# A hybrid encoder layer: which ring of buffers a pair's expert choices use, where the expert activations are loaded, integer positions, and late gate steps with priority

## The chip, the cores and the metric

The kernel runs on one core of one Trainium2 chip. The metric is the device time of one execution in microseconds (us), the median of several runs. The profile is a trace of one execution. Its engines are PE (TensorE's matmuls; PEld its weight loads), DVE (VectorE), ACT (ScalarE), POOL (GpSimd) and SP (SyncE, which here only issues transfers). Each runs its instructions in program order.

## The reference

One layer: a token-mixing part (convolution and RWKV-7 heads), then a retrieval of single-neuron experts. The cut below is the second part, in which the change lies; S = D = 1024, 8 heads, 128 keys per half, 16 choices per head, 16384 experts.

```python
h2 = adaln(x, shift2, scale2)
q = (h2 @ peer_wq).reshape(bsz, seq, PEER_HEADS, PEER_QDIM)
s1 = jnp.einsum('bshd,hnd->bshn', q[..., :half], peer_k1)
s2 = jnp.einsum('bshd,hnd->bshn', q[..., half:], peer_k2)
v1, i1 = lax.top_k(s1, PEER_TOPK)
v2, i2 = lax.top_k(s2, PEER_TOPK)
cand = (v1[..., :, None] + v2[..., None, :]).reshape(bsz, seq, PEER_HEADS, PEER_TOPK * PEER_TOPK)
sc, ci = lax.top_k(cand, PEER_TOPK)
experts = (jnp.take_along_axis(i1, ci // PEER_TOPK, axis=-1) * PEER_NKEYS
           + jnp.take_along_axis(i2, ci % PEER_TOPK, axis=-1))
gates = jax.nn.softmax(sc, axis=-1)
u_sel = jnp.take(peer_u, experts, axis=0)
act = jax.nn.gelu(jnp.einsum('td,tkd->tk', h2, u_sel), approximate=False) * gates
y2 = jnp.einsum('tk,tkd->td', act, jnp.take(peer_v, experts, axis=0))
x = layer_norm(ALPHA * x + gate2[:, None, :] * y2, ln2_g, ln2_b)
```

## The kernel before

Tokens go in eight tiles of 128, and through the middle of the kernel in four pairs of tiles (256 tokens). Up to about 530 us the modulation and the input projection run, then the RWKV recurrence over 16 chunks, into which work of the pairs that are done is filled. For a pair, `front` is the output projection (L186, evicted by ACT at L796) and the layer norms, and `query` computes the queries: `to_channels` turns the normed tokens into `h2hi` and `h2lo` (PE L220, ACT L222), then come 16 query tiles in four groups of four. A query tile is 24 matmuls (L186) with a 1 MB block of split weights, `wsplit`, which `load_split` loads at L170 into one of three buffers; ACT evicts it as `qt` (L858). After each group PE forms the key scores (L863) from the group's four evictions, and ACT evicts them (L866).

For tiles 0 to 5, `choose` then finds the 16 experts of each head from the scores. DVE forms the candidates (L904) and searches them (L767 to L771); ACT copies the positions from integers to floats (L912); DVE turns positions into two indices (L913 to L930, L955, L958 to L960); ACT casts indices (L935) and takes the exp (L956); DVE compares (L940) and POOL multiplies and sums (L943, L949, L951) to pick the chosen keys, and `put` sends them to `sel_d` (L932). Choices take their tiles of 2 KB ("pages") from a ring: up to here the ring `pg`, of 31 pages, which the query's `qt`, `s12`, keys and `hf` use as well.

Tiles 0 to 4 are handled densely: `gate_matrix` reads `sel_d` back (L973), transposes it (L979), and in 32 steps of four tokens builds a matrix of gates over all experts (DVE L991 and L995, POOL L997, ACT L1000 and L1001, PE L1003, eviction L1004), written to `G_d` by DMA (L1011). Tiles 5 to 7 gather their experts' rows by DMA. The expert loop (32 groups of experts) multiplies the 640 dense tokens' activations `h2h` and `h2l` with the expert weights (L1227), applies gelu and gates (L1229 to L1233), multiplies back (L1261) and adds up (L1266), beside which POOL and DVE work through the gathers (L1145, L1153, L1160). The choices of tiles 6 and 7 run there too (`choose_late`).

Between recurrence and expert loop lies a loop (L1067 on) that steps the last pair's `front`, the third pair's `query` and the last pair's `query`, with a step of the choices every second pass and a step of the gates every twelfth (`TSLOW`, `TGATE`). The last pair's `front` takes its pages from a second ring, `pg2`, of 20 pages (`NP2`). Behind the loop that ring is closed, and its memory goes to the pool `dp` with `h2h` and `h2l`, which 16 transfers (L1080) load from `h2t_d`.

The order of each engine's instructions is not written out: a scheduler with a time model lists them as their inputs come ready in the model, in order of priority, and this order is then fixed.

Of the kernel before, what the change touches and what calls it, by code (L numbers as in the profile page):

```python
# [10 lines left out]
F32 = mybir.dt.float32  # L11
F32R = mybir.dt.float32r
BF = mybir.dt.bfloat16
I32 = mybir.dt.int32
U32 = mybir.dt.uint32
AF = mybir.ActivationFunctionType
OP = mybir.AluOpType
# [4 lines left out]
S = 1024  # L22
D = 1024
KD = 8
CW = 512
KS = 31
NH = 8
# [13 lines left out]
PB = 256  # L41
# [13 lines left out]
WRAW = 2  # L55
WSPLIT = 3
RUN = 4
NP2 = 20
PIN = 3
STEPS = 4, 3  # L60
# [20 lines left out]
def layer_kernel(ctx, tc, x, cols, c_row, cond_w, w_in, w2a2, g2, w_out, ln_rows, wq, keys, peer_u, peer_ut, peer_v, peer_vt, out):  # L81
    nc = tc.nc
    V, A, G, T = nc.vector, nc.scalar, nc.gpsimd, nc.tensor
    ld = nc.sync.dma_start
# [26 lines left out]
    dt = lambda shape, name, n: [dram.tile(shape, F32, name=f"{name}{i}") for i in range(n)]  # L111
# [9 lines left out]
    h2t_d = dram.tile([2, KD, 128, ND], F32, name="h2t_d")  # L121
    sel_d = dt([3, 128, 128], "sel_d", 8)
    score_d = {t: [dram.tile([128, 512], F32, name=f"score_d{t}_{g}") for g in range(4)] for t in range(6, 8)}
    split_d = {}

    GPART = [(0, ND // TB - 4), (ND // TB - 4, ND // TB - 1), (ND // TB - 1, ND // TB)]
    G_d = [dram.tile([32, 128, b - a, 4 * TB], F32, name=f"G_d{a}") for a, b in GPART]
# [28 lines left out]
    def page(name, dt=F32, w=512):  # L156
        return pgp.tile([128, max(w, 512)], dt, tag="pg", name=name)[:, :w]
# [6 lines left out]
    def load_split(src, j):  # L164

        both = ws.tile([128, 2, KD, 128], F32R, name="wsplit", bufs=WSPLIT)
        hi, lo = both[:, 0], both[:, 1]
        key = src.tensor.name, j
        if key in split_d:
            ld(both.bitcast(F32), split_d[key])  # L170
        else:
            raw = load_raw(src[j])
            A.activation(hi, raw, AF.Copy)  # L173
            G.tensor_sub(lo, raw, hi.bitcast(F32))  # L174
            split_d[key] = dram.tile([128, 2, KD, 128], F32, name=f"split_{key[0]}{j}")
            ld(split_d[key], both.bitcast(F32))
        return hi, lo
# [50 lines left out]
    def step(jobs):  # L228
        while jobs:
            try:  # L230
                next(jobs[0])
                return
            except StopIteration:
                jobs.pop(0)
# [212 lines left out]
    slow, gates, gb, conv_left, psg, selbank = [], [], [], [], [], [None]  # L447
# [108 lines left out]
    for l in range(6):  # L556
# [6 lines left out]
        nm = rc.tile([128, 64], F32, name=f"offm{l}", bufs=1)  # L563
# [9 lines left out]
    side, rate, credit, fills = [], [0.0], [0.0], [0]  # L573

    def fill():

        credit[0] += rate[0]
        fills[0] += 1
        if credit[0] >= RUN:
            credit[0] -= RUN  # L580
            for _ in range(RUN):
                step(side)
# [9 lines left out]
            fn(hi_, q)  # L592
            fill()

    kept, ys, late, normed = {}, {}, [], {}

    def quad(name, bufs=3):
        return rw.tile([128, 4, 64], F32, name=name, bufs=bufs)
# [229 lines left out]
    def query(t0):  # L828

        n, nt, tile0 = PB, PB // 128, t0 // 128  # L830
        fetch = [tile0 + t in GT for t in range(nt)]
        xn = normed.pop(t0)
        hi, lo = duo("h2hi", F32R)[1], duo("h2lo", F32R)[1]

        def keep(k, h, l):
            for w, f in enumerate((h, l)):
                for t in range(nt):
                    if not fetch[t]:
                        d = 128 * DT.index(tile0 + t)
                        ld(h2t_d[w, k, :, d:d + 128], f[:, 128 * t:128 * t + 128].bitcast(F32))  # L840

        to_channels(xn, lambda k: mod[:, 24 + k:25 + k], lambda k: modp[:, k, 1:2], hi, lo, keep)
        yield
        vi = [page("vi").rearrange("p (q h a r) -> p q h a r", q=2, h=NH, a=2) for t in range(nt)
              if tile0 + t not in score_d]
        val = [t[:, 0] for t in vi]
        idx = [t[:, 1].bitcast(U32) for t in vi]
        for g in range(4):
            kt = pgp.tile([128, 4, 128], F32, tag="pg", name="keys")
            ld(kt, keys[:, 4 * g:4 * g + 4, :])  # L850
            qt = []
            for m in range(4):
                w = load_split(wq, 4 * g + m)
                pt = mm(n)
                yield from proj(w, (hi, lo), pt)
                if m % 2 == 0:
                    qp = page("qt").rearrange("p (a t) -> p a t", a=2)
                A.activation(qp[:, m % 2, :], pt, AF.Copy)  # L858
                qt.append(qp[:, m % 2, :])
            for t in range(nt):  # L860
                ps = mm()
                for m in range(4):
                    T.matmul(ps[:, 128 * m:128 * m + 128], qt[m][:, 128 * t:128 * t + 128], kt[:, m, :],  # L863
                             start=True, stop=True)
                s = page("s12")
                A.activation(s, ps, AF.Copy)  # L866
                if tile0 + t in score_d:
                    ld(score_d[tile0 + t][g], s)
                    yield
                    continue  # L870
                for m in range(4):
                    best16(val[t][:, 2 * g + m // 2, m % 2], idx[t][:, 2 * g + m // 2, m % 2], s[:, 128 * m:128 * m + 128])
                    yield
        for t in range(len(vi)):
            slow.append(choose(tile0 + t, val[t], idx[t], 0, NH, 4, lambda nm, d, w: page(nm, d, w), G))

    def choose_late(tt, lt):

# [10 lines left out]
    def choose(tt, val, idx, h0, nh, nb, new, E):  # L889
# [2 lines left out]
        sh3 = [128, nh, TOPK]  # L892
        quad = lambda nm, dt=F32: new(nm, dt, 4 * n).rearrange("p (q h r) -> p q h r", q=4, h=nh)
        qf, qg, qu = quad("tkf"), quad("tkg"), quad("tku", U32)
        fp, m1, m2, m3 = (qf[:, i] for i in range(4))
        top, shf, fo = qg[:, 0], qg[:, 1], (qg[:, 2], qg[:, 3])
        pos = qu[:, 0]
        shi, qi_, ri_ = (qu[:, i].bitcast(I32) for i in (1, 2, 3))
# [10 lines left out]
                best16(top[:, h], pos[:, h], cand[:, h - hh, :])  # L909
                yield  # L910

        A.activation(fp, pos, AF.Copy)  # L912
        V.tensor_scalar(m1, fp, 32.0, None, op0=OP.is_ge)  # L913
        V.tensor_scalar(m2, fp, 48.0, None, op0=OP.is_ge)
        V.tensor_scalar(m3, fp, 64.0, None, op0=OP.is_ge)
        yield
        V.tensor_add(shf, m1, m2)
        V.scalar_tensor_tensor(shf, m3, 2.0, shf, op0=OP.mult, op1=OP.add)
# [8 lines left out]
        qb = new("tkb", BF, 8 * n).rearrange("p (q h r) -> p q h r", q=8, h=nh)  # L927
        isel, jsel = qb[:, 0], qb[:, 1]
        V.scalar_tensor_tensor(isel, m1, -2.0, qi_, op0=OP.mult, op1=OP.add)
        V.tensor_sub(jsel, fp, ri_)  # L930
        yield
        put = lambda w, t: ld(sel_d[tt][w][:, h0 * TOPK:h0 * TOPK + n], t.rearrange("p h r -> p (h r)"))  # L932
        for half, sel in ((0, isel), (1, jsel)):
# [125 lines left out]
    selbank[:] = [selx.enter_context(tc.tile_pool(name="pss", bufs=1, space=PSUM, side="right")), psum]  # L1059
    pg2x = ExitStack()  # L1060
    pg2 = pg2x.enter_context(tc.tile_pool(name="pg2", bufs=NP2, side="right"))

    def page2(name, dt=F32, w=512):
        return pg2.tile([128, max(w, 512)], dt, tag="pg2", name=name)[:, :w]

    side += [front(S - PB, page2), query(S - 2 * PB), query(S - PB)]
    while side or slow or gates:  # L1067
        step(side)
        fills[0] += 1
        if fills[0] % TSLOW == 0 or not side:  # L1070
            slow_step(1)
        if fills[0] % TGATE == 0 or not side:
            step(gates)

    pg2x.close()
    dp = ctx.enter_context(tc.tile_pool(name="dp", bufs=1, side="right"))
    h2h, h2l = ([dp.tile([128, ND], F32R, name=f"h2{w}{k}") for k in range(KD)] for w in "hl")
    for k in range(KD):
        for w, h in enumerate((h2h, h2l)):
            ld(h[k].bitcast(F32), h2t_d[w, k])  # L1080
    selx.close()
    fex.close()
    dl = ctx.enter_context(tc.tile_pool(name="dl", bufs=1))
# [38 lines left out]
    late = {t: choose_late(t, lt) for t in score_d}  # L1122
# [86 lines left out]
    for g in range(32):  # L1209
# [4 lines left out]
        for e in range(4):  # L1214
# [7 lines left out]
            for bs in NBLK:  # L1222
                p = md(NW) if g == 0 and e < 3 and bs.start else mg(NW)
                i = 0
# [23 lines left out]
        for half in range(2):  # L1248
# [3 lines left out]
            for t in range(NT):  # L1252
# [3 lines left out]
                p = md()  # L1256
# [73 lines left out]
```

## Time and profile before

| what | value |
|---|---|
| median of 3 runs | 3269.81 us (3268.62 to 3273.45) |
| profiled execution, its own time | 3266.04 us |
| its span, first to last instruction | 3264.3 us |
| mean granted TensorE clock | 0.946 of full |
| TensorE busy in the 25 us from 1300, 1325, 1350, 1375, 1400 | 22.63, 7.08, 19.61, 23.09, 24.91 us |
| TensorE busy in the 25 us from 1200 | 15.28 us |
| first matmul of the expert loop | 1408.26 us |

Rows of the timeline read: start, duration, engine, line, operation, output<-inputs, shapes, and in brackets the idle time of the engine before it with what ended it. Names like `wsplit` and `tkf` are those of the program.

### The profile page before, as it was taken

How to read it: one execution, taken by the hardware profiler on the slowest of the kernel's cores; microseconds unless marked ns; L12 is line 12 of the kernel's file. 1: busy time of each engine (PE TensorE's matmuls, PEld its weight loads, DVE VectorE, ACT ScalarE, POOL GpSimd, SP SyncE). 2: the span in 40 equal slices, each digit the busy share in tenths (PEclk: the TensorE clock that was granted, in tenths of full speed). 3: DMA queues.
4: the chain of work that ended last, by engine and by line, in shares of the span. 5: the costliest groups of instructions: out<-in, count | busy, mean ns of one | idle time of the engine just before them, and what ended most of it. 6: DMA issues, size and time to landing. Idle time of an engine off the chain costs nothing.

```text
span 3264.3 us, 54847 instructions
## 1 busy us (share of the span) xinstructions
PE 3033.4 (93%) x20400; PEld 2641.4 (81%) x20400; DVE 2524.4 (77%) x5588; ACT 1206.7 (37%) x2358; POOL 1822.8 (56%) x1448
## 2 busy tenths in 40 slices
PE   6968999999888689699999999999999999999995
PEld 4735667688778679698988998888999999999995
DVE  6379566747778878658999998998778777777878
ACT  5562453343255476272323232232322232222322
POOL 2410112224433654458777877677777778787872
PEclk9979899979779899799999999999999999999998
DMA  8876464458449689879998989899999999999994
GB/s 307 293 213 225 136 192 138 138 192 295 148 149 309 228 268 323 286 238 365 320 348 311 350 317 329 301 324 355 328 353 328 346 328 349 334 344 336 337 342 180
DMA packets 412364, 922.25 MB, mean 283 GB/s; under 512 B 81808, under 2 KB 222400, under 8 KB 390080
## 3 DMA queue, kind: packets, MB, share of 16 engines
q1 hardware_dynamic: 219264, 474.10, 42.0%
q0 software_dynamic: 110592, 402.70, 33.6%
q10 hardware_dynamic: 82240, 41.94, 4.6%
q8 instruction: 160, 2.62, 0.3%
q14 instruction: 108, 0.88, 0.1%
HBM read 788.58 MB, written 130.05 MB: 281 GB/s over the span
## 4 chain that ended last, share of the span: by engine, by line
PE 39%; DVE 12%; issue 5%; DMA 3%; POOL 2%; ACT 1%; ACTq 0%; POOLq 0%; DVEq 0%
PE mg L1227 18%; PE md L1261 18%; DVE grow L1153 2%; PE mm L186 2%; DVE gy L1160 2%; PE mgate L1003 1%; DVE yacc L1266 1%; POOL grow L1145 1%; DMA vraw<-peer_vt 1%; DMA grow<-peer_v,eid 1%; POOL vlo L1188 1%; DMA grow<-peer_u,eid 1%; POOL ulo L1188 1%; DMA G_d<-stage 0%; DVE mg L1231 0%
## 5 line engine op out<-in xcount | busy, mean ns | idle before, releaser
L1227 PE MATMUL mg<-h2h,uhi 128*128 128x320 f32 x2024 | 626.9, 310 | 8.7 <-DVE al L1233 8.7
L1227 PE MATMUL mg<-h2l,uhi 128*128 128x320 f32 x2024 | 625.7, 309 | 0.0
L1227 PE MATMUL mg<-h2h,ulo 128*128 128x320 f32 x2024 | 625.5, 309 | 0.0
L1160 DVE SCALAR_TENSOR_TENSOR gy<-grow,gz,gy 128x1024 f32<-128x1024 f32 x381 | 488.0, 1281 | 16.8 <-DMA grow<-peer_v,eid 12.0
L1261 PE MATMUL md<-vhi,al 128*128 128x512 f32 x1280 | 498.1, 390 | 0.3 <-DVE al L1233 0.3
L1261 PE MATMUL md<-vlo,ah 128*128 128x512 f32 x1280 | 496.9, 390 | 0.0
L1261 PE MATMUL md<-vhi,ah 128*128 128x512 f32 x1280 | 492.5, 391 | 4.2 <-ACT ah L1232 3.1
L1153 DVE SCALAR_TENSOR_TENSOR grow<-grow,gh 128x1024 f32<-128x1024 f32 x384 | 460.7, 1212 | 39.1 <-DMA grow<-peer_u,eid 34.6
L1145 POOL DMA_INDIRECT grow<-peer_u,eid x384 | 364.7, 950 | 192.9 <-DVE grow L1153 73.6
L1145 POOL DMA_INDIRECT grow<-peer_v,eid x384 | 363.3, 946 | 182.4 <-DVE gy L1160 81.5
L1227 PEld LDWEIGHTS mg<-h2h,uhi 128*128 128x128 f32 x2024 | 380.4, 188 | 17.3 <-DVE al L1233 12.6
L1227 PEld LDWEIGHTS mg<-h2l,uhi 128*128 128x128 f32 x2024 | 380.5, 188 | 5.0
L1227 PEld LDWEIGHTS mg<-h2h,ulo 128*128 128x128 f32 x2024 | 380.5, 188 | 3.1
L1188 POOL TENSOR_TENSOR ulo<-uraw,uhi 128x1024 fp32r<-128x1024 f32 x128 | 309.4, 2417 | 31.0 <-ACT uhi L1186 23.3
L1188 POOL TENSOR_TENSOR vlo<-vraw,vhi 128x1024 fp32r<-128x1024 f32 x128 | 309.5, 2418 | 25.1 <-ACT vhi L1186 22.3
L1266 DVE TENSOR_TENSOR yacc<-md,yacc 128x512 f32<-128x512 f32 x310 | 211.0, 685 | 109.0 <-PE md L1261 102.2
L1261 PEld LDWEIGHTS md<-vhi,ah 128*128 128x128 f32 x1280 | 239.5, 188 | 53.6 <-ACT ah L1232 6.4
L1261 PEld LDWEIGHTS md<-vlo,ah 128*128 128x128 f32 x1280 | 240.3, 188 | 48.8
L1261 PEld LDWEIGHTS md<-vhi,al 128*128 128x128 f32 x1280 | 240.3, 188 | 45.4 <-DVE al L1233 0.5
L1186 ACT ACTIVATE vhi<-vraw 128x1024 fp32r<-128x1024 f32 x128 | 135.2, 1056 | 380.7 <-DMA vraw<-peer_vt 324.4
L174 POOL TENSOR_TENSOR wsplit<-wraw,wsplit 128x1024 fp32r<-128x1024 f32 x46 | 113.0, 2458 | 255.7 <-ACT wsplit L173 249.7
L997 POOL TENSOR_TENSOR ob<-ob,selt 128x384 f32<-128x384 f32 x160 | 136.5, 857 | 209.4 <-DVE ob L995 142.3
(404 smaller groups left out, 6092.2 us busy)
## 6 DMA issues: line engine op xcount, KB each, us to landing
uraw<-peer_ut SPq DMA_DIRECT2D x128, 512.0 KB
vraw<-peer_vt SPq DMA_DIRECT2D x128, 512.0 KB
wsplit<-split_wq SPq DMA_DIRECT2D x48, 1024.0 KB
G_d<-stage ACTq DMA_DIRECT2D x20, 2048.0 KB
gmat<-G_d SPq DMA_DIRECT2D x32, 1024.0 KB
cw<-cond_w SPq DMA_DIRECT2D x48, 512.0 KB
wsplit<-split_w_out SPq DMA_DIRECT2D x24, 1024.0 KB
split_w_in<-wsplit SPq DMA_DIRECT2D x22, 1024.0 KB
```

The source lines that it names most:

```text
L174: G.tensor_sub(lo, raw, hi.bitcast(F32))
L186: T.matmul(pt, l[:, k, :], r[k], start=i == 0, stop=i == 3 * KD - 1)
L997: G.tensor_mul(ob[:, :3], ob[:, :3], gt[:, ts.start:ts.start + 3, None].to_broadcast([128, 3, 128]))
L1003: T.matmul(pt[:, t, :], ob[:, t, :], oa[:, t, :], start=True, stop=True)
L1145: G.indirect_dma_start(out=r, out_offset=None, in_=peer_u if k < 128 else peer_v, in_offset=bass.IndirectOffsetOnAxis(ap=eid[:, k % 128:k ...
L1153: V.scalar_tensor_tensor(r, r, 1.0, ht, op0=OP.mult, op1=OP.mult, accum_out=z[:, i:i + 1])
L1160: V.scalar_tensor_tensor(y, r, z[:, i - 128:i - 127], y, op0=OP.mult, op1=OP.add)
L1186: A.activation(hi, raw, AF.Copy)
L1188: G.tensor_sub(lo, raw, hi.bitcast(F32))
L1227: T.matmul(p, l[:, k, :], r[k][:, bs], start=i == 0, stop=i == 3 * KD - 1)
L1261: T.matmul(p, l[:, ts], r[:, e % 2, :], start=e == 0 and q == 0, stop=e == 3 and q == 2)
L1266: ins = V.tensor_add(ya, p, ya)
```

## The change

Four edits. The ring's constructor `page2` becomes an entry of a list, so that `query` can reach it, and the choices of the third pair (tiles 4 and 5) take their ten pages each from it in place of `pg`. `load_split` keeps its DMA instructions in `fetched`, and the 16 loads of `h2h` and `h2l` are issued after the one that belongs to `('wq', 10)`, the 11th query tile, of the last pair. In `choose`, ACT's copy of the positions to floats goes; DVE's comparisons read the integers, and `jsel` is formed by one operation with an integer input in place of a subtraction. The steps of the gates in the last loop get a priority raised by 500.

```diff
+HP = 'wq', 10
+GPRI = 500
+P2C = 1
...
-    split_d = {}
+    split_d, fetched = {}, {}
...
         if key in split_d:
-            ld(both.bitcast(F32), split_d[key])
+            fetched[key] = ld(both.bitcast(F32), split_d[key])
...
-            slow.append(choose(tile0 + t, val[t], idx[t], 0, NH, 4, lambda nm, d, w: page(nm, d, w), G))
+            slow.append(choose(tile0 + t, val[t], idx[t], 0, NH, 4, lambda nm, d, w, p=page2[0] if t0 == S - 2 * PB and P2C else page: p(nm, d, w), G))
...
-        fp, m1, m2, m3 = (qf[:, i] for i in range(4))
+        m1, m2, m3 = (qf[:, i] for i in range(3))
...
-        A.activation(fp, pos, AF.Copy)
-        V.tensor_scalar(m1, fp, 32.0, None, op0=OP.is_ge)
-        V.tensor_scalar(m2, fp, 48.0, None, op0=OP.is_ge)
-        V.tensor_scalar(m3, fp, 64.0, None, op0=OP.is_ge)
+        place = pos.bitcast(I32)
+        V.tensor_scalar(m1, place, 32.0, None, op0=OP.is_ge)
+        V.tensor_scalar(m2, place, 48.0, None, op0=OP.is_ge)
+        V.tensor_scalar(m3, place, 64.0, None, op0=OP.is_ge)
...
-        V.tensor_sub(jsel, fp, ri_)
+        V.scalar_tensor_tensor(jsel, place, 1.0, ri_, op0=OP.mult, op1=OP.subtract)
...
-            step(gates)
+            with tc.high_priority(offset=GPRI) if GPRI else nullcontext():
+                step(gates)
...
-    for k in range(KD):
-        for w, h in enumerate((h2h, h2l)):
-            ld(h[k].bitcast(F32), h2t_d[w, k])
+    with tc.issue_after(fetched[HP].ins) if HP else nullcontext():
+        for k in range(KD):
+            for w, h in enumerate((h2h, h2l)):
+                ld(h[k].bitcast(F32), h2t_d[w, k])
```

The changed file's lines lie three further down from the first hunk on: L170 is L173, L186 L189, L858 L861, L932 L935, L956 L959, L1003 L1006, L1080 L1083, L1227 L1230.

The order changes in three places that matter here. The first is SyncE's queue at the last pair's query. Before, the last four of the 16 loads and what follows them, the weights of query tiles 3 to 6 and tile 4's gates:

```order
L1080 DMA h2h_14485<-h2t_d 128x640
L1080 DMA h2l_14493<-h2t_d 128x640
L1080 DMA h2h_14486<-h2t_d 128x640
L1080 DMA h2l_14494<-h2t_d 128x640
L170 DMA wsplit<-split_wq_6268 128x2048
L170 DMA wsplit<-split_wq_6357 128x2048
L170 DMA wsplit<-split_wq_6391 128x2048
L932 DMA sel_d_119<-tkg 128x128
L170 DMA wsplit<-split_wq_6424 128x2048
```

Now, the end of that query in the same queue: the puts of tile 4's sums (`sel_d_119`) and of tile 5's (`sel_d_120`), the weights of query tiles 13, 14 and 15, and the first of the 16 loads:

```order
L935 DMA sel_d_119<-tkg 128x128
L173 DMA wsplit<-split_wq_6771 128x2048
L935 DMA sel_d_119<-tkg 128x128
L173 DMA wsplit<-split_wq_6804 128x2048
L976 DMA selr<-sel_d_119 128x128
L853 DMA keys<-keys 128x512
L871 DMA score_d_2_125<-s_14153 128x512
L871 DMA score_d_2_129<-s_14161 128x512
L976 DMA selr<-sel_d_119 128x128
L935 DMA sel_d_120<-tkg 128x128 x2
L173 DMA wsplit<-split_wq_6838 128x2048
L1083 DMA h2h_14473<-h2t_d 128x640
```

The loads moved from ahead of query tile 3's weights to behind those of the last one, tile 15, and the weights of tiles 13 to 15 stand behind puts.

The second is ACT in the same query, from the last activations of `to_channels` on, with both choices of the third pair. Before:

```order
L223 ACTIVATE h2hi<-hf 128x256
L912 ACTIVATE tkf<-tku 128x128
L935 ACTIVATE tkb<-vi 128x128 x2
L956 ACT_TABLE_LOAD
L956 ACTIVATE tkg<-tkg 128x128
L858 ACTIVATE qt<-mm 128x256 x3
L912 ACTIVATE tkf<-tku 128x128
L935 ACTIVATE tkb<-vi 128x128 x2
L956 ACTIVATE tkg<-tkg 128x128
L858 ACTIVATE qt<-mm 128x256
L866 ACTIVATE s_13634<-mm 128x512
```

Now, from the same place:

```order
L226 ACTIVATE h2hi<-hf 128x256
L861 ACTIVATE qt<-mm 128x256 x2
L938 ACTIVATE tkb<-vi 128x128 x2
L959 ACT_TABLE_LOAD
L959 ACTIVATE tkg<-tkg 128x128
L861 ACTIVATE qt<-mm 128x256 x2
L869 ACTIVATE s_13628<-mm 128x512
L869 ACTIVATE s_13650<-mm 128x512
L861 ACTIVATE qt<-mm 128x256 x2
L938 ACTIVATE tkb<-vi 128x128 x2
L959 ACTIVATE tkg<-tkg 128x128
L861 ACTIVATE qt<-mm 128x256 x2
```

The exp of tile 4 moved behind two evictions of query tiles, and that of tile 5 from behind three to behind six.

The third is PE where the expert loop begins, with the last query tile, the last key scores and tile 4's gate steps (four matmuls a step). Before; twelve more gate matmuls stand inside the last query tile, 17 rows further up:

```order
L1003 MATMUL mgate<-oa,ob 128x128 x4
L186 MATMUL mm<-h2hi,wsplit 128x256
L863 MATMUL mm<-keys,qt 128x128
L1003 MATMUL mgate<-oa,ob 128x128 x4
L863 MATMUL mm<-keys,qt 128x128
L1003 MATMUL mgate<-oa,ob 128x128 x4
L863 MATMUL mm<-keys,qt 128x128 x6
L1003 MATMUL mgate<-oa,ob 128x128 x12
L1227 MATMUL md<-h2h_14479,uhi 128x320
```

Now, with none further up:

```order
L189 MATMUL mm<-h2hi,wsplit 128x256
L866 MATMUL mm<-keys,qt 128x128
L1006 MATMUL mgate<-oa,ob 128x128 x4
L866 MATMUL mm<-keys,qt 128x128
L1006 MATMUL mgate<-oa,ob 128x128 x4
L866 MATMUL mm<-keys,qt 128x128
L1006 MATMUL mgate<-oa,ob 128x128 x4
L866 MATMUL mm<-keys,qt 128x128 x5
L1006 MATMUL mgate<-oa,ob 128x128 x12
L1230 MATMUL md<-h2h_14473,uhi 128x320
```

Ahead of the loop stand 24 gate matmuls in place of 36; the twelve others come inside the loop. In both, 22 matmuls of the loop's first block run before the next gates. Earlier, in the third pair's query, gate matmuls of the tiles before stand 16 to 20 ahead of where they stood, counted against the query tiles, from its first score group on; at its end the counts are equal, 512 of tiles 0 to 3.

More of the change, by code (lines that the diff above doesn't have):

```diff
@@ L593, in pairs @@
             fill()
-    kept, ys, late, normed = {}, {}, [], {}
+    kept, ys, late, normed, page2 = {}, {}, [], {}, []
     def quad(name, bufs=3):
@@ L1061, in layer_kernel @@
     pg2 = pg2x.enter_context(tc.tile_pool(name="pg2", bufs=NP2, side="right"))
-    def page2(name, dt=F32, w=512):
-        return pg2.tile([128, max(w, 512)], dt, tag="pg2", name=name)[:, :w]
-    side += [front(S - PB, page2), query(S - 2 * PB), query(S - PB)]
+    page2.append(lambda name, dt=F32, w=512: pg2.tile([128, max(w, 512)], dt, tag="pg2", name=name)[:, :w])
+    side += [front(S - PB, page2[0]), query(S - 2 * PB), query(S - PB)]
     while side or slow or gates:
```

## The prediction

> **What bounds the kernel now.** I read the busy shares first, then TensorE's waits in the last stage, then its waits and the table of stretches just before, then the timelines of that place.
>
> ```profile
> PE 3033.4 (93%) x20400; PEld 2641.4 (81%) x20400; DVE 2524.4 (77%) x5588; ACT 1206.7 (37%) x2358; POOL 1822.8 (56%) x1448
> PE mg L1227 <- DVE al L1233: 8.7, 9, 1.7
> ```
>
> The first line is the page's busy time, the second TensorE's longest wait from 1450 us to the end (in total, times, longest). Over 1800 us that is next to nothing: the expert loop is bound by TensorE, and the run ends a fixed time after that loop gets under way. Time is to be won ahead of it, where TensorE idles:
>
> ```profile
> PE mm L186 <- DMA wsplit<-split_wq: 14.1, 2, 12.2
> PE mm L863 <- ACT qt L858: 11.4, 1, 11.4
> 1325.00:1350.00 25.00, 7.08 (x36) 6.92 (x36) 23.53 (x86) 3.12 (x8) 16.15 (x13) 0.65 0.74 290
> ```
>
> Two rows of its waits from 1300 to 1460 us, and one of the stretches (length, then PE, PEld, DVE, ACT, POOL busy, the granted clock, DMA share, GB/s). The last pair's query loses 14.1 + 11.4 = 25.5 us. In that stretch PE is busy for 7.08 us of 25, DVE for 23.53, so DVE is what I watch when a wait goes.
>
> ```profile
> 1336.95 0.55 PE L186 MATMUL mm<-h2hi,wsplit 128*128 128x256 f32 x1 [12.22 <-DMA wsplit<-split_wq]
> 1355.39 1.23 PE L863 MATMUL mm<-keys,qt 128*128 128x128 f32 x4 [11.37 <-ACT qt L858]
> 1313.03 0.32 SPq L1080 DMA_DIRECT2D h2h<-h2t_d  x1
> 1327.77 0.32 SPq L1080 DMA_DIRECT2D h2l<-h2t_d  x1
> 1328.64 1.97 SPq L170 DMA_DIRECT2D wsplit<-split_wq  x3
> h2h<-h2t_d SPq DMA_DIRECT2D x8, 320.0 KB
> ```
>
> TensorE's two long waits in its timeline; in the sync queue's, the first and last of the 16 loads of expert activations and the query weights behind them; and from the list of DMAs the size of one load. The weights of query tile 3 stand behind 16 x 320 KB = 5.24 MB. The second wait has another cause:
>
> ```profile
> 1328.28 0.31 ACT L912 ACTIVATE tkf<-tku 128x128 f32<-128x128 uint32 x1 [12.99 <-DVE tku L771]
> 1330.30 0.31 ACT L956 ACTIVATE tkg<-tkg 128x128 f32<-128x128 f32 x1
> 1330.52 0.91 ACT L858 ACTIVATE qt<-mm 128x256 f32<-128x256 f32 x3
> 1354.16 0.31 ACT L912 ACTIVATE tkf<-tku 128x128 f32<-128x128 uint32 x1 [22.73 <-DVE tku L771]
> 1354.78 0.29 ACT L956 ACTIVATE tkg<-tkg 128x128 f32<-128x128 f32 x1
> 1354.98 0.36 ACT L858 ACTIVATE qt<-mm 128x256 f32<-128x256 f32 x1
> 1330.64 0.28 DVE L958 TENSOR_REDUCE sm<-tkg 128x8 f32<-128x128 f32 x1 [1.32 <-ACT tkg L956]
> 1354.17 0.29 DVE L955 TENSOR_TENSOR tkg<-tkg,mx 128x128 f32<-128x128 f32 x1
> ```
>
> ACT's and DVE's timelines. ACT runs in order, and ahead of the query evictions L858 it has a choice's copy of the positions (L912) and its exp (L956). These wait for DVE, which ends tile 4's search at 1328.28 and tile 5's at 1354.16; between the two DVE rows it has no further gap.
>
> **The change, part by part.** *Positions as integers.* The copy goes, but the exp behind it stays and waits for L955, the next thing on DVE, and three comparisons (L913 to L915) now stand ahead of L955. ACT gives back 0.31 us, DVE takes three operations of at most 0.29. No row shows a comparison that reads integers; the nearest are L955's 0.29 and L912's 0.31, so I bound the edit between -1 and +1 us over the kernel and take nothing. The same pair stands ahead of the evictions of the last pair's projection:
>
> ```profile
> 1124.46 0.58 PE L186 MATMUL mm<-ychi,wsplit 128*128 128x256 f32 x1 [10.83 <-ACT y L796]
> ```
>
> That wait stays as it is, since the exp still stands there behind the same search. In the expert loop the copies of the late choices go, beside a TensorE that is full: nothing.
>
> *Loads behind the query, pages in the other ring.* Tile 3 loses its 12.22 us wait. I then follow TensorE through the four groups of four query tiles, with rows of the chain (start, length), of GpSimd's timeline and of the stretches:
>
> ```profile
> 1356.62 13.01 PE mm L186 x96
> 1371.41 2.89 PE mm L186 x24
> 1374.32 7.50 DMA wsplit<-split_wq
> 1385.06 1.34 PE mm L863 x12
> 1395.80 2.68 PE mgate L1003 x24
> 1398.48 2.75 PE mm L186 x23
> 1369.34 0.30 POOL L951 TENSOR_TENSOR tkg<-oh 128x64 f32<-128x64 bf16 x1
> 1372.10 0.30 POOL L951 TENSOR_TENSOR tkg<-oh 128x64 f32<-128x64 bf16 x1
> 1377.54 1.10 POOL L951 TENSOR_TENSOR tkg<-oh 128x64 f32<-128x64 bf16 x4
> 1372.00:1392.00 20.00, 18.09 (x153) 17.92 (x152) 0.00 (x0) 3.92 (x10) 6.64 (x15) 1.00 1.00 353
> ```
>
> A warm query tile takes 2.89 us; the four behind the second wait took 13.01, which is 1.45 more than four warm ones. Tile 2 ends at 1336.95 - 12.22 = 1324.7, so tile 3 now ends at 1327.6. Two of its group's evictions stand behind tile 4's exp, at about 1329.4; the scores begin near 1330.1 (a wait of 2.5) and take 1.2, and tiles 4 to 7 end at 1342.9. The next scores need two evictions behind tile 5's exp. That still waits for DVE, which wins only about 1.0 us of the 1.32 that it waited for tile 4's exp: exp at about 1354.1, scores from 1354.9. **So the second wait doesn't go; it is some 12 us and sits four tiles later**, and the gain is the four tiles that are done ahead of it. Scores and tiles 8 to 11 end at 1354.9 + 1.2 + 13.0 = 1369.1 where they ended at 1385.06: 16 us.
>
> In the last group the weights come late. In the sync queue the two puts of tile 4's sums now stand ahead of the weights of tiles 13 and 14, and both puts of tile 5's ahead of tile 15's. GpSimd ended these sums at 1369.6, 1372.4 and 1378.6; with DVE they come 1.0 earlier. A tile's 1.05 MB takes 3.0 us at the last row's 353 GB/s, and 7.50 in the full queue of the chain's row; I take 4.5, nearer the lower end since little else is queued. Weights 13 and 14 are then in at 1372.9 and 1375.9, in time for a TensorE that gets there at 1373.3 and 1376.2; weights 15 leave at 1377.6 and land at 1382.1, 3 us late. Tile 15 ends at about 1385.5. It ended at 1401.23, or 1398.6 without the gates in between: 13 us are left.
>
> *The start of the expert loop.* The order puts the 16 loads behind the sixteenth query tile's weights, not the eleventh's: 6.29 MB from 1377.6 on. The same bytes went out from 1313.03 and were in when tile 3 began at 1336.95: 23.9 us, or 264 GB/s. At 353 GB/s they take 17.8. The last load lands between 1395.4 and 1401.5; between ends this near I take the middle, 1398.4. Nothing hides what is left of them after tile 15 but the gates of tile 4:
>
> ```profile
> 1408.26 0.39 PE L1227 MATMUL md<-h2h,uhi 128*128 128x320 f32 x1
> 1411.57 1.16 PE L1003 MATMUL mgate<-oa,ob 128*128 128x128 f32 x9
> 1428.41 0.59 ACT L1004 ACTIVATE stage<-mgate 128x512 f32<-128x512 f32 x1
> 1429.57 0.59 ACT L1004 ACTIVATE stage<-mgate 128x512 f32<-128x512 f32 x1
> ```
>
> The first 22 rows of the loop ran from 1408.26 to 1411.57, behind nine gate steps (36 rows of four tokens a step); the ACT rows give 1.16 us a step. Now six steps stand ahead of them, and the rows end with the last load, at 1398.6. Three steps follow later, 3.5 us. Gain 1411.6 - 1398.6 - 3.5 = 9.5 us. By the ends of the load it is 6.5 to 12.4; were the loads no bound at all, tile 15, six steps and 3.3 us would end at 1395.8, gain 12.3. **I take 9.5**: of the 13 us, 3.5 are given back to the loads.
>
> [...]
>
> *Late gates put forward.* In the third pair's query they move ahead by about five steps (16 to 20 rows), into a place where TensorE waits anyway:
>
> ```profile
> PE mm L220 <- ACT hf L222: 5.3, 4, 3.5
> PE mgate L1003 <- POOL ob L997: 3.3, 4, 2.0
> ```
>
> These are its waits from 1200 to 1240. A step is 2.68 / 3 = 0.9 us on TensorE, so five steps in idle time save at most 4.5. But each also puts three operations of together 1.16 us on ACT, ahead of the evictions L222 for which TensorE waits there: if they stand ahead of three of the four, 3 us are lost. I take +2. By the end of that query the count of gates is what it was, so nothing is carried on but this.
>
> *Sum.* 9.5 + 2 = 11.5 us. The profiled execution took 3266.04 (span 3264.3), 3.8 below the median of the three, 3269.81; so 3254.5 on that basis, **3258.3** as a median.
>
> **The rivals.** *A, both waits go.* If tile 5's search ended before 1342.9 and the loads found idle queues, the 25.5 us would go, with 2 for the gates: about 3242. Against it: DVE was busy without a gap up to 1354.17, and its work is the same. Chance 0.08.
>
> *B, the gain is given back at the loop's start.* The loads do not go where the change says they go, so they can arrive late. With the slow landing (6.5), the gates at their lower end (-3) and the integers at theirs (-1), 2.5 us are left: 3267. Any gain from 6.5 down to -6.5 belongs here, 0.2% or about what a measurement of this kernel can tell from no change. For it: the 264 GB/s is the only measured time of these very loads. Against it: they then shared the engines with tile weights more than they now will. Chance 0.24.
>
> *C, slower: the queue is held by GpSimd.* Weights 15 and all 16 loads stand behind tile 5's puts, and the loads also need its pages back, which GpSimd frees last. What it takes longer is lost one for one. With the two gains of the sum, 11.5, it evens out when the last load lands at 1409.9, that is when the weights leave at 1386.0 at the slow rate, 8.4 us after what I take. At 1392.6, 15 us after, the kernel is 6.6 slower, 3276.4, and up to 3281 where the gates lose 3 too. For it:
>
> ```profile
> 1358.08 2.24 POOL L943 TENSOR_TENSOR oh<-oh,tkb 128x1024 bf16<-128x1024 bf16 x1 [8.31 <-ACT s L866]
> ```
>
> GpSimd's first product for tile 5, after 8.31 us without work: a chain that starts so late has no slack to give. Against it: GpSimd's order here is the one of before, and DVE, which feeds it, is not later. Chance 0.12, with the other ways in which the earlier stages' new order could lose as much.
>
> **How the numbers follow.** The forecast, a gain of 6.5 to 16 us, has 0.56. Faster than 3263.3 are the forecast and A: 0.64. Within 0.2% is B: 0.24. Slower than 3276.3 is C: 0.12. The forecast's own bounds are 9.5 (6.5 to 12.4), 2 (-3 to 4.5), 0 (-1 to 1), so 2.5 to 17.9 us: 3252 to 3267. The range reaches on into A and through B, to **3245 to 3275**, and leaves out most of A and C, just under 0.2.
>
> **What would show it.** Right: query tile 3 with no wait for its weights; one wait of 10 to 14 us for L858's successor ahead of the scores of the second group, around 1343 to 1355; a wait of 2 to 5 us for the last query weights near 1380; the first rows of the loop drawn out by the loads until about 1398; the wait of 10.8 near 1124 still there. Wrong: the wait for DVE is gone or the loop begins before 1392 (A); the last load lands after 1405 (B); GpSimd ends tile 5's sums after 1386 (C); or the wait near 1124 has changed, or the third pair's query begins more than 5 us earlier or later, so that the time was won or lost in stages that I cost at nothing.

## The result, and the profile after

| | before | changed |
|---|---|---|
| median of the first comparison | 3268.62 us (3262.59 to 3273.45, 5 runs) | 3241.49 us (3237.15 to 3247.30, 5 runs) |
| ratio | | 0.9919 [0.9901, 0.9936] |
| profiled execution, its span | 3266.04, 3264.3 us | 3241.49, 3239.7 us |
| first matmul of the last pair's query | 1313.38 us | 1302.08 us |
| first matmul of the expert loop | 1408.26 us | 1378.42 us |
| from the first of these to the end of the span | 1950.9 us | 1937.6 us |

The kernel became faster by more than forecast: 27 us by the medians, where 10.3 to 11.5 were forecast and the range ended at 3245. Two more comparisons of the same order of instructions, told below, give 0.9945 [0.9924, 0.9965] and 0.9945 [0.9919, 0.9971]. All 20 executions of it have a median of 3245.6 us (3237.15 to 3262.38), so the first five were among the faster ones, and 18 to 27 us is what the three comparisons show.

The rows that answer to those of before are two of TensorE's waits from 1250 to 1460 us, the same stretch of the table, and TensorE's timeline; the last row but one is the first matmul of the expert loop, the last one stands where before had its wait of 10.83 us for ACT in the last pair's projection:

```profile
PE mm L189 <- DMA wsplit<-split_wq: 9.4, 4, 2.9
PE mm L866 <- ACT qt L861: 0.3, 1, 0.3
1325.00:1350.00 25.00, 20.62 (x169) 19.98 (x167) 14.76 (x82) 4.26 (x12) 21.09 (x22) 1.00 0.88 312
1302.08 0.58 PE L189 MATMUL mm<-h2hi,wsplit 128*128 128x256 f32 x1 [0.38 <-ACT hf L225]
1315.72 0.35 PE L189 MATMUL mm<-h2hi,wsplit 128*128 128x256 f32 x1 [2.60 <-DMA wsplit<-split_wq]
1349.09 0.35 PE L189 MATMUL mm<-h2hi,wsplit 128*128 128x256 f32 x1 [2.95 <-DMA wsplit<-split_wq]
1365.67 0.55 PE L189 MATMUL mm<-h2hi,wsplit 128*128 128x256 f32 x1 [2.72 <-DMA wsplit<-split_wq]
1378.42 0.39 PE L1230 MATMUL md<-h2h,uhi 128*128 128x320 f32 x1
1107.16 0.58 PE L189 MATMUL mm<-ychi,wsplit 128*128 128x256 f32 x1 [5.07 <-ACT y L799]
```

Of the two waits of 12.2 and 11.4 us, the first is down to 2.60 and **the second is gone: 0.3**. What is left are weights that come 1.1 to 3.0 us late, each time for the last tile of a group of four (tiles 3, 7, 11 and 15). The wait in the last pair's projection, near 1124 us in before, has halved to 5.07. ACT's and SyncE's timelines show the two exps, the last query weights and the first and last of the 16 loads:

```profile
1314.22 0.31 ACT L959 ACTIVATE tkg<-tkg 128x128 f32<-128x128 f32 x1 [1.10 <-DVE tkg L958]
1335.12 0.31 ACT L959 ACTIVATE tkg<-tkg 128x128 f32<-128x128 f32 x1 [6.42 <-DVE tkg L958]
1359.42 0.38 SPq L173 DMA_DIRECT2D wsplit<-split_wq  x1
1363.27 0.32 SPq L1083 DMA_DIRECT2D h2h<-h2t_d  x1
1373.37 0.32 SPq L1083 DMA_DIRECT2D h2l<-h2t_d  x1
```

Tile 5's exp comes 33.0 us after the query begins; before, it was 41.4 (1354.78 against 1313.38). The last load is issued at 1373.37 and lands at 1379.9, 1.5 us after the loop's first matmul, and TensorE shows no wait for the loads.

### The profile page after: what moved, and what is told of

The parts are those of the page before. It is cut to its first block, busy times and chain, and to the rows that moved or that the text cites. A ratio compares the mean times of both kernels' runs of the same rounds, so it can differ in the third digit from the quotient of the medians.

```text
span 3239.7 us, 54819 instructions
## 1 busy us (share of the span) xinstructions
PE 3029.2 (94%) x20400; PEld 2639.4 (81%) x20400; DVE 2519.6 (78%) x5588; ACT 1204.1 (37%) x2344; POOL 1822.6 (56%) x1448
## 4 chain that ended last, share of the span: by engine, by line
PE 44%; DVE 11%; DMA 3%; issue 3%; POOL 2%; ACT 1%; ACTq 0%; POOLq 0%; DVEq 0%
PE mg L1230 20%; PE md L1264 20%; DVE grow L1156 2%; PE mm L189 2%; PE mgate L1006 2%; DVE gy L1163 1%; DVE yacc L1269 1%; DMA grow<-peer_v,eid 1%; DMA vraw<-peer_vt 1%; DMA grow<-peer_u,eid 1%; POOL grow L1148 1%; POOL vlo L1191 0%; DMA wsplit<-split_wq 0%; POOL ulo L1191 0%; DVE mg L1234 0%
## 5 line engine op out<-in xcount | busy, mean ns | idle before, releaser
L1230 PE MATMUL mg<-h2h,uhi 128*128 128x320 f32 x2024 | 626.9, 310 | 6.0 <-DVE al L1236 5.9
L1230 PE MATMUL mg<-h2l,uhi 128*128 128x320 f32 x2024 | 625.8, 309 | 0.0
L1230 PE MATMUL mg<-h2h,ulo 128*128 128x320 f32 x2024 | 625.8, 309 | 0.0
L1163 DVE SCALAR_TENSOR_TENSOR gy<-grow,gz,gy 128x1024 f32<-128x1024 f32 x381 | 488.4, 1282 | 14.4 <-DMA grow<-peer_v,eid 12.3
L1230 PEld LDWEIGHTS mg<-h2h,uhi 128*128 128x128 f32 x2024 | 380.7, 188 | 14.7 <-DVE al L1236 10.1
L1230 PEld LDWEIGHTS mg<-h2l,uhi 128*128 128x128 f32 x2024 | 380.6, 188 | 5.1
L1230 PEld LDWEIGHTS mg<-h2h,ulo 128*128 128x128 f32 x2024 | 380.5, 188 | 3.1
L1191 POOL TENSOR_TENSOR ulo<-uraw,uhi 128x1024 fp32r<-128x1024 f32 x128 | 309.2, 2416 | 31.3 <-ACT uhi L1189 29.5
```

The lines of the kernel that those rows point to most:

```text
L1163: V.scalar_tensor_tensor(y, r, z[:, i - 128:i - 127], y, op0=OP.mult, op1=OP.add)
L1230: T.matmul(p, l[:, k, :], r[k][:, bs], start=i == 0, stop=i == 3 * KD - 1)
```

## The experiments

All times of stages below are read from the timelines. "To the end" runs from the first matmul of the last pair's query to the end of the span. The end of a search is read at the start of DVE's subtraction behind it (L955, now L958). In the expectations of no_late, no_gates, no_pages and float_pos, theory 1 has the surplus over the forecast come from DVE, which ends the third pair's two choices sooner, and theory 2 from the stages before the last two pairs, by their new order.

### One order, executed again

The rule that puts the loads behind the 11th query tile turned out to change nothing: without it the order of every engine is the same.

```diff
-HP = 'wq', 10
+HP = None
```

> The change without the rule that puts the loads behind the 11th query tile; pages, integers and gates as changed. The order of every engine is then the same as in the changed kernel, since the loads wait for the pages of the third pair's choices anyway. Both theories: no difference, ratio to the kernel before within 0.002 of 0.9919. [...]

> The changed kernel itself, a third profile of one order. Stretch from the last pair's query to the end: 1937 to 1940 us, tiles 4 and 5 with unblocked compares (0.69 us each), as in the other two. Its time falls within the 3237 to 3260 of the 11 executions so far; against the kernel before 0.991 to 0.9955.

> The kernel before itself, so that its profile is taken a second time. The stretch from the first matmul of the last pair's query to the end took 1950.9 us in the first profile of this order, 1937.6 and 1938.8 in two of the changed order. If what an edit does in that stretch can be read from one profile, it is 1950 to 1952 here, though all that comes before may be 5 to 15 us longer or shorter.

| execution | profiled span | query begins | tile 4's, tile 5's search ends after it | to the end | ratio of the comparison |
|---|---|---|---|---|---|
| before | 3264.3 | 1313.4 | 14.9, 40.8 | 1950.9 | |
| before_again | 3266.9 | 1310.8 | 14.9, 40.8 | 1956.1 | 0.9996 [0.9981, 1.0012] |
| changed | 3239.7 | 1302.1 | 11.8, 32.7 | 1937.6 | 0.9919 [0.9901, 0.9936] |
| no_late | 3258.4 | 1319.6 | 11.8, 32.7 | 1938.8 | 0.9945 [0.9924, 0.9965] |
| after_again | 3249.5 | 1311.5 | 11.8, 32.7 | 1938.0 | 0.9945 [0.9919, 0.9971] |

Three executions of one order begin that query at 1302, 1312 and 1320 us, and then agree to 1.2 us up to the end. The two of before differ there by 5.2: before_again was to show 1950 to 1952 us if one profile is enough, and showed 1956.1. So a difference of 11 us at 1302, which I could have taken for a gain in the earlier stages, can't be told from scatter, and a difference of less than some 5 us to the end can't be read from single profiles either; the searches agree to 0.1 us. The ratio of no_late was expected within 0.002 of 0.9919 and lies 0.0026 above, with overlapping intervals. One source of the scatter shows in two 5 us pieces of the same chain of matmuls, in no_late first and then in the changed kernel (stretch, length, busy PE, PEld, DVE, ACT, POOL, the granted clock, DMA share, GB/s):

```profile
815.00:820.00 5.00, 5.00 (x28) 4.32 (x24) 5.00 (x29) 1.26 (x2) 3.10 (x3) 0.50 0.28 80
805.00:810.00 5.00, 5.00 (x44) 4.41 (x45) 4.18 (x23) 1.26 (x2) 2.58 (x2) 0.98 0.02 5
```

At a clock of 0.50 TensorE gets through 28 matmuls, at 0.98 through 44; the two pieces are not matmul for matmul the same. Around this place, from 776 to 812 us of the changed kernel, no_late falls back by 4.1 us, and it has 10 us more at half clock. Where such a spell falls differs from run to run, though the instructions are the same.

### Each edit alone

Here one edit is made and the others left out: the rings (`P2C = 1` alone), the integer positions, or the priority of the gates (`GPRI = 500` alone).

> The kernel before with one edit, the third pair's choices on the last pair's ring; the loads then stand behind the last query tile's weights by themselves. [...] Theory 2 (the gain needs the integers or the gates as well): above 1947, within 4 us of the kernel before.

> The kernel before with one edit, the integer positions. Theory 1: nothing in the last stage, 1949 to 1956 us from the last pair's query to the end as in the two profiles of before; ahead of it the new order of the scheduler may move a few us. If the 8 us that the changed kernel is ahead between the first pair's query and the third's come from this edit, that stretch takes 488 to 498 us here, in place of 501.7 and 503.4; in all 3260 to 3264. Theory 2 (the integers are worth nothing anywhere): 500 to 504 us there, 3266 to 3270 in all.

> The kernel before with one edit, the priority of the gate steps. By the forecast: 2 us faster in the third pair's query (84 in place of 86.1 and 84.7), no change elsewhere. By what the changed kernel showed against the one without the priority (90 to 92 against 83.6 in that stretch, given back in the stretch behind it): 88 to 93 us there, and some 5 less from the last pair's query to the end; in all within 3 us of the kernel before either way.

| kernel | median | ratio | tile 4's, tile 5's search | to the end | four compares of tile 4, of tile 5 |
|---|---|---|---|---|---|
| only_pages | 3255.3 (12) | 0.9962 [0.9948, 0.9977] | 10.3, 36.2 | 1939.4 | 6.2, 4.7 us |
| only_int | 3258.4 (10) | 0.9978 [0.9965, 0.9992] | 14.8, 39.1 | 1952.0 | 6.1, 2.7 us |
| only_gates | 3260.7 (10) | 0.9983 [0.9967, 0.9999] | 15.5, 41.4 | 1949.5 | 6.2, 4.7 us |

The ring alone gives most of the last stage, and it moves the loads by itself: the memory of that ring is what the loads go to, and the choices now hold it to the end of the query. It does one thing that I had not seen. With pages free, DVE starts on tile 4's candidates ahead of the query, not in it. The first such rows of before, and two of only_pages:

```profile
1318.53 0.56 DVE L904 TENSOR_TENSOR cand<-vi 128x128 f32<-128x128 f32 x3
1308.97 0.38 DVE L907 TENSOR_TENSOR cand<-vi 128x64 f32<-128x64 f32 x2
```

The row of before is 5.1 us after the query's first matmul, that of only_pages 3.2 us ahead of it (1312.2). Tile 4's search ends 4.6 us sooner against the query, and tile 5's with it. TensorE's remaining wait for the second group's evictions is 3.4 us in only_pages, not the 12 of the forecast. With blocked compares (2.40 us in place of 0.69) I had expected 1942 to 1944 us to the end; it is 1939.4.

The integers alone are worth 7 us by the medians, none of it seen in the last stage. The gates alone: 5 us by the medians, at the edge of their interval, and 1 to 7 by the last stage, which is no more than the scatter there. Both change the order of the engines well ahead of the last stage. Two readings of the profiles, sorted by order up to the third pair's query (the ring changes nothing there), are the stretch from the first query eviction of the first pair to that of the third, and the wait of 10.8 us near 1124 that the forecast watched:

| positions, gates | stretch, us | wait near 1124, us |
|---|---|---|
| floats, no priority (before, before_again, only_pages) | 501.7, 503.4, 498.4 | 10.8, 10.1, 9.8 |
| floats, priority (only_gates, float_pos, float_noprod) | 499.4, 488.8, 494.4 | 5.6, 5.4, 6.1 |
| integers, no priority (only_int, no_gates, int_sub_nogates) | 494.0, 490.7, 496.2 | 5.9, 4.9, 5.5 |
| integers, priority (changed, no_late, after_again, no_pages, int_sub, int_noprod) | 491.9, 498.0, 493.0, 494.2, 488.4, 496.2 | 5.1, 4.7, 5.5, 5.6, 4.8, 7.1 |

One order alone scatters by up to 11 us in that stretch. The wait scatters less: it falls from some 10 us to 5 to 7 with either edit, and no further with both. This fits that each is worth some us alone and that either can be missed there; why the new orders shorten the wait was not followed up.

### Each edit taken away

```diff
-GPRI = 500
+GPRI = 0
...
-P2C = 1
+P2C = 0
```

The first line is no_gates, the second no_pages. float_pos brings back ACT's copy and the float comparisons of before.

> The change without the priority of the gate steps; all else as changed. [...] Theory 2 (the surplus is won in the stages before the last two pairs, by their new order): nothing but the forecast's 2 us, about 3243. By the forecast itself: 3243.

> The change with the third pair's choices on the ring of before; loads put behind the 11th query tile, integers and gates as changed. The loads then stand behind query tile 10's weights and not behind the last ones. Theory 1: DVE's third compare of tile 4 and 5 is blocked again (2.4 us in place of 0.69), the search of tile 5 ends about 5 us later against the query's begin; the loads lie beside the query and hold tiles 11 to 15 back by up to 8 us, but the loop starts without them; about 3248 us. Theory 2: within 2 us of the changed kernel, 3241. By the forecast's terms: the loads cost no 3.5 us at the loop but tile weights wait longer, 3243 to 3250.

> The change with the positions copied to floats by ACT as before; pages, loads and gates as changed. Theory 1: the integers are worth nothing, within 1 us of the changed kernel, 3241 to 3242.5. Theory 2: the new order of the stages before the third pair comes from the missing copies, so these stages are back to before; 5 to 8 us later, 3247 to 3249.

| kernel | median | ratio | tile 4's, tile 5's search | to the end |
|---|---|---|---|---|
| no_gates | 3242.5 (6) | 0.9922 [0.9900, 0.9944] | 10.6, 31.5 | 1937.5 |
| no_pages | 3267.2 (12) | 0.9996 [0.9980, 1.0013] | 16.0, 40.3 | 1958.6 |
| float_pos | 3251.0 (12) | 0.9960 [0.9942, 0.9979] | 11.4, 37.4 | 1942.9 |

Without the ring nothing is left of the gain. There the loads do stand behind the 11th query tile, among the last weights, and TensorE waits:

```profile
PE mm L189 <- ACT s L869: 14.3, 1, 14.3
PE mm L189 <- DMA wsplit<-split_wq: 6.9, 2, 5.9
PE mm L189 <- ACT qt L861: 5.5, 1, 5.5
```

These are its waits in no_pages from 1312 to 1425. ACT's evictions stand behind the searches as before, and the loads stand among the weights, which come late. Every expectation for this kernel, 3241 to 3250 us, was missed. The priority of the gates can be left out at no loss: I had given it 2 us. Without the integers the median is 5.4 us above the 3245.6 of the changed order, which is within the scatter of so many executions; both theories of float_pos missed, since its stages ahead of the third pair are as fast as the changed kernel's. What is clear is the last stage: there the integers let tile 5's search end 4.7 us sooner (37.4 and 32.7), and TensorE's wait for the second group's evictions is 5.4 us in float_pos and 0.3 in the changed kernel. The end comes 4 to 5 us sooner, about as much as the scatter there.

### Why the integers count: DVE beside GpSimd

Between the two searches DVE forms four compares, then tile 5's candidates. The same eight rows in before and in the changed kernel, with GpSimd's first product:

```profile
1332.79 5.92 DVE L940 TENSOR_TENSOR oh<-iota_q,tkb 128x1024 bf16<-128x1024 bf16 x4
1338.64 6.04 DVE L904 TENSOR_TENSOR cand<-vi 128x128 f32<-128x128 f32 x4
1333.62 2.23 POOL L943 TENSOR_TENSOR oh<-oh,tkb 128x1024 bf16<-128x1024 bf16 x1 [28.34 <-DVE oh L940]
1316.44 2.49 DVE L943 TENSOR_TENSOR oh<-iota_q,tkb 128x1024 bf16<-128x1024 bf16 x4
1318.85 2.42 DVE L907 TENSOR_TENSOR cand<-vi 128x128 f32<-128x128 f32 x4
1317.26 3.95 POOL L946 TENSOR_TENSOR oh<-oh,tkb 128x1024 bf16<-128x1024 bf16 x1 [30.09 <-issue]
```

In before GpSimd's product takes 2.23 us, up to 1335.85, and DVE's third compare, begun beside it, ends at 1336.39: 2.40 us in place of 0.69. The fourth takes 2.40 as well and ends 0.55 us after GpSimd's next product. In the changed kernel it is the other way round: DVE's four compares run through at 0.69 each, and GpSimd's product takes 3.95, where the next one takes 1.91; it ends at 1321.21, beside tile 5's fourth candidate, which takes 1.94 up to 1321.26. So each is held up beside the other in these rows; by what was not shown. To see whether this is all that tells floats and integers apart, GpSimd's products and sums of tile 4 were left out, with zeros in their place, in the version with float positions and in the changed one:

```diff
+                if tt == 4:
+                    E.memset(fo[half][:, hs], 0.0)
+                    continue
                 E.tensor_mul(oh, oh, ib[:, hs, :, None].to_broadcast(sh4))
```

> The change with float positions (whose compares of tiles 4 and 5 are blocked), and GpSimd's products and sums of tile 4 left out: zeros stand in the chosen keys of tile 4. If the blocked compares are GpSimd's doing, the four compares of tile 4 take 2.7 us in all and the searches of tiles 4 and 5 lie clearly less than 20.9 us apart, since the candidates of tile 5 aren't blocked either: 15 to 18. If DVE's compares are slow by themselves with float positions (their operands, their pages), 6.2 us and above 23.

> The changed kernel with GpSimd's products and sums of tile 4 left out in the same way. [...]

```profile
1323.75 2.49 DVE L943 TENSOR_TENSOR oh<-iota_q,tkb 128x1024 bf16<-128x1024 bf16 x4
1326.16 0.65 DVE L907 TENSOR_TENSOR cand<-vi 128x128 f32<-128x128 f32 x4
```

These are the DVE rows of float_noprod, 2.49 and 0.65 us where float_pos has 5.93 and 6.07: the slow compares are GpSimd's doing. The searches lie 15.4 us apart there and 14.5 in int_noprod, where they lay 25.9 and 20.9 apart with GpSimd at work. So its work costs DVE 10.5 us with floats and 6.4 with integers. Of the 5.0 us between the versions, 4.1 are what GpSimd's work costs the one more than the other and 0.9 DVE's own. Each of these two versions was executed once.

What decides which of the two is held up is open. I tried the form of the instruction ahead of the compares, with the order otherwise the same:

```diff
-        V.scalar_tensor_tensor(jsel, place, 1.0, ri_, op0=OP.mult, op1=OP.subtract)
+        V.tensor_sub(jsel, place, ri_)
```

> The changed kernel with one operation in another form: jsel as a subtraction of two integers in place of the operation with a scalar. The order of every engine is the same otherwise. [...]

It isn't that: the searches lie 20.9 us apart, not 25.9, and the ratio is 0.9914 [0.9887, 0.9941], no different from the changed kernel. To the end it takes 1933.0 us, below the 1937 to 1940 that I expected of no effect, though the order is the changed kernel's: another sign of some 5 us of scatter there. Which of the two it is was the same in each execution of one order and differs between orders: in before DVE is blocked in all six choices (a compare of 2.40 us in each), in the changed kernel in the first three (0.69 for every compare of the others), in no_gates in the first two. Nor is it the integers as such: with them and without the ring (only_int, no_pages) tile 4's compares are blocked (6.1 us for the four in only_int), and with floats and the priority (only_gates, float_pos) those of tile 2 are not. For tiles 4 and 5 it took the ring and the integers together.

### Weights out of GpSimd's way, and a best version

```diff
-        put = lambda w, t: ld(sel_d[tt][w]
+        put = lambda w, t: (G.dma_start if E is G and w < 2 else ld)(sel_d[tt][w]
```

> The changed kernel with the four puts of the sums issued by GpSimd, which makes them, in place of SyncE: the weights of query tiles 13 to 15 no longer stand behind them. Theory 1 (in the last query group the weights are late because of the puts): TensorE's two waits for weights there, 5.7 us together, are gone; the loads still wait for the pages, so the loop's first rows now wait for them by up to as much; 2 to 6 us faster than the changed kernel from the last pair's query to the end, 1932 to 1936. Theory 2 (the weights are late because the transfers are slow there): the waits stay, no gain; where GpSimd's own issue holds up its sums, slower.

> The changed kernel with the puts on GpSimd's queue and without the priority of the gates: the version that should be the fastest if both readings hold. Theory 1: 83 to 85 us in the third pair's query, 1932 to 1936 from the last pair's query to the end, 5 to 10 us less than the changed kernel in all, 3232 to 3240. Theory 2: as the changed kernel, 3241 to 3250.

Neither is faster than the changed kernel: 3250.6 us, 0.9956 [0.9940, 0.9972], and 3248.5, 0.9949 [0.9931, 0.9967]. To the end they take 1936.7 and 1934.1 us, too near to the changed order's 1933 to 1939 to tell. In puts_pool the puts no longer stand ahead of the weights, and the weights are late all the same:

```profile
PE mm L189 <- DMA wsplit<-split_wq: 7.3, 4, 2.4
PE mm L866 <- ACT qt L861: 2.0, 1, 2.0
SPq L173 <- PE mm L189: 35.5, 12, 13.9
```

(TensorE's waits from 1311 to 1395, and the longest of SyncE's.) Tile 15 waits 1.7 us there, against 2.7, 1.3 and 1.9 in the three profiles of the changed order, and the other waits fall on tiles 3, 7 and 11 in both. So the puts are not what the late weights chiefly hang on. The third row points to something that neither theory has: a tile's weights can be issued only when TensorE is through with the tile three before and one of the three buffers is free. In the changed kernel they then take 4.8 to 8.7 us to land, while the two tiles in the other buffers last 5.8. More buffers were not tried. The last try joined the two variants that were no slower, the integer subtraction and no priority:

> The changed kernel with jsel as an integer subtraction and without the priority of the gates, the two variants of it that were no slower. If the priority is worth nothing: 3238 to 3246 us, 0.990 to 0.9935 of the kernel before, the third pair's query in 83 to 85 us. If it is worth the 5 us that it showed alone: 3243 to 3251.

It is level with the changed kernel: 3240.5 us, 0.9920 [0.9898, 0.9942]. No version clearly beats it; the ring and the integers carry what there is.

## Why the prediction was wrong

The direction and the place of the chief gain were right, and so was what the ring does to the loads; the second wait, the worth of the integers and the size were not. By its own steps, counted from the query's first matmul (1313.38 in the forecast, 1302.08 in the profile after):

| step | forecast | measured |
|---|---|---|
| tile 3's wait for weights | 0 | 2.6 |
| tile 5's exp | 40.7 | 33.0 |
| TensorE is ready for the second group's scores | 29.5 | 32.8 |
| wait of the second group's scores | 12 | 0.3 |
| tile 11 ends | 55.7 | 50.2 |
| tile 15's weights are issued | 64.2 | 57.3 |
| tile 15 ends | 72.1 | 69.1 |
| the last load lands | 85.0 | 77.9 |
| the loop's first 22 rows end | 85.2 | 79.5 |

**The step that failed first** is "that still waits for DVE, which wins only about 1.0 us", with its ground in rival A, "its work is the same". DVE won 8.1 us (40.8 to 32.7), in two parts: 3 to 4.6 since tile 4's candidates start before the query, where free pages allow it, and 5.0 with the integers, of which 4.1 are time that DVE loses beside GpSimd's work without them. So the exp comes 7.7 us sooner. That is most of the 11.7 us by which the wait fell short of the forecast; some 3.3 are TensorE's own lateness, since the forecast let tiles 3 to 7 run without a wait for weights, and tiles 3 and 7 waited 2.6 and 1.1 us. I had rows of both kinds before me, candidates of 0.56 us for three alone and of 6.04 for four beside GpSimd, and took DVE's durations as fixed. Rival A, both waits gone, is what came nearest: the loop begins 76.3 us after the query, ahead of its sign (78.6), though its condition was not met, as the search of tile 5 ended at 32.7 and not before 29.5. With float positions, the searches lie 25.9 us apart as I assumed, and to the end float_pos gains 8.0 us and only_pages 11.5 on the profile that the forecast was made from, around its 9.5 (on before_again 5.2 more).

**Positions as integers, "I take nothing"** was the wrong term: 7 us alone, and a wait of 5.4 us in the last stage when taken away. The reason I gave, that the exp stands behind the same search, was right as far as ACT goes. **"That wait stays as it is"**, said of the 10.8 us near 1124, failed as well: it is 4.7 to 5.5 us in the three profiles of the changed order. This was one of the forecast's signs that time is won in stages it costs at nothing.

**The loads** cost nothing: the loop began at 1378.42 without a wait. The forecast let them hold up the first rows until 85 us after the query's begin, 3.5 of the 13 us. Their transfer was priced well: from the issue of tile 15's weights to the landing of the last load it took 20.5 us, where 20.8 were forecast, 307 GB/s and between the bounds of 264 and 353. It began 6.9 us sooner, since the puts of tile 5's sums, behind which it stands, follow the search that ended sooner. The last load landed 1.6 us before the first 22 rows ended, so there is little slack.

**The end** comes only 13.3 us sooner (on the forecast's profile), though the 22 rows end 18.7 us sooner against the query: the loop gives back 5.4 us, where the forecast set 3.5 aside for the three gate steps. From its first matmul the loop takes 1861.3, 1864.9 and 1861.8 us in the changed order, 1856.0 and 1859.6 in before.

**The gates, "+2"**, can't be found where they were placed. From its first eviction to the last pair's first matmul, the third pair's query takes 86.1 and 84.7 us in before, 91.6, 90.9 and 89.9 in the changed order, which is slower, and 83.6 in no_gates; in the pair puts_pool and puts_nogates it is the other way round, 86.1 with the priority and 91.5 without. The whole is no slower without it.

**The sum.** Of the 27 us of the first comparison 11.5 were forecast. About 4 us are that the first five executions were fast ones, 4 to 9 more than forecast were won in the last stage, by which profile of before is taken, and the rest lies ahead of it, where single profiles scatter too much to place it.

**Right** were the first wait, which the moved loads took from 12.2 to 2.6 us, the six gate steps ahead of the loop, the place of the loads behind the last query tile, and the time of their transfer. Tile 15's weights come late as forecast, by 1.3 to 2.7 us, but that is partly luck: the same wait hits tiles 7 and 11, for which it was not forecast. The profiled basis added to the miss: I took single executions at 0.2%, and 20 executions of one order spread over 25 us.

## What to carry to other kernels

A wait that "only moves" rests on the other engine's durations, and where a third engine worked beside that one, these were no constants here (0.69 and 2.40 us for one form of compare): look for the same instruction at two durations in one trace, and price the step by both. Where tiles come from a ring, ask not only who waits for a page but what could start earlier with one free. Execute the same order two or three times before reading a stage's difference: what agrees between them can be an effect of the order, and what doesn't is scatter.

## What the hardware showed beyond that

The half-clock spells fall differently in each execution of one order of instructions. In the traces of before and of the changed kernel the granted clock has only two values, 0.50 and 1.00 (62 and 64 records), so its mean gives their sum: some 2 x (1 - 0.946) x 3264 = 353 us of before and 317 of the changed kernel's first profile (0.951), and, read the same way, 332 and 325 of its two others (0.949, 0.950). How much of the scatter this makes is open: between the changed kernel's first profile and no_late, 15 us more at half clock go with a span that is 18.7 us longer, while the two profiles of before have the same mean (0.946) and spans 2.6 us apart.
